# A one-core decoder layer: mixer C beside the stick-breaking passes, mixer A after them, and new tile pools

## Chip, core and metric

The kernel runs on one core of one Trainium2 chip. The metric is the device time of one execution in microseconds (us). Before the change it is 2517.34 us, the median of 3 runs (2516.91 to 2517.41).

## What is computed

One layer of a decoder over 2048 tokens of width 1024, in float32 throughout. Products that need full precision are made of high and low parts (three products with fp32r operands for one). The mixing half, cut to what matters here:

```python
h = _rmsnorm(x, norm_mix[l])
a_u, a_v, b_in, c_q, c_k, c_v, d_q, d_k, d_v = jnp.split(h @ w_in[l], splits, axis=-1)
y_a = _chunked_sgu(a_u, a_v, sgu_w[l], sgu_b[l])          # gelu, layer norm per head, 128x128 causal mix, gate
y_b = _multiscale_pool(b_in, pool_w[l], pool_scale[l])    # trailing means of 2, 4, 8, 16 tokens
y_c = _swa_sink_attention(c_q, c_k, c_v, swa_sinks[l], rel_bias)   # window of 128, softmax with a sink
y_d = _stick_breaking_attention(d_q, d_k, d_v)            # sigmoid(z) times a running product, causal, 4 heads
x = x + _rmsnorm(jnp.stack([y_a, y_b, y_c, y_d], 2), gain).reshape(B, S, D) @ w_out[l]
```

After it comes the feed-forward half: `x + (silu(h Wg) * (h Wu)) Wd` with its own normalisation, and a last normalisation.

## The kernel before

**Pieces.** The tokens stand in 4 chunks of 512 (c), 8 pieces of 256 (s) and 16 blocks of 128 (b). `stick(c, pair, q)` is one pass of the stick-breaking attention: the queries of one chunk and of one pair of heads (0 and 1, then 2 and 3) against all key chunks up to it. Its loop over head, key chunk and block makes a score tile z on PE (L302, L303), two sigmoids on ACT (L306, L309), on the diagonal two masks on POOL (L312), a running product pr by a scan on DVE (L315), the weights s (L320), their transposes tr on PE (L330), the high and low parts wt on ACT and DVE (L332, L333), and the products acc with the values (L341, L342). `finish` copies out a head's result (ysb, L353). There are eight passes, n = 0 to 7.

**What runs beside the passes.** `feed` is a generator that issues all other projections and mixers A, B and C; it yields after each step with a cost. `merge(main, fill, ratio)` takes one pass and, after each of its yields, as many steps of `feed` as `ratio` times the pass's cost. `upto(limit)` hands out steps up to a chunk mark. Marks 0 to 3 make keys, queries, values and mixer B for the first pair; from mark 4 on, `keys_queries` makes those of the second pair. Before the change `gate` places mixer A (`mixer_a`, `sgu`: a projection of 512 columns, `gelu`, a layer norm, four products m with the gate's weights, the store of u) beside passes 3 to 5; after mark 8 come mixer C's projections (st, stored in cd) and `attend(mixer_c())`, whose steps `swa(s)` load keys kr and queries qr, split them (ck on ACT and DVE, cq on POOL), make logits z into `block` (L447), take the maximum and the exponentials (L467), transpose them (trc), multiply with the values (o) and store. The few steps of it that fit run beside passes 6 and 7.

**After the passes.** `load_wo` loads the output weights by row group (oraw) and splits them into 16 tiles wo (L618 on ACT, L619 on DVE). `out_proj` goes over 16 blocks: `prepare` loads y (the four mixers' outputs) and xres, normalises y per mixer (squares L644, L648) and transposes it (`split_T`, L630, L632, L633); 48 products ops follow (L694 to L696), and the residual is added (L697); `finish` normalises the row for the feed-forward half, transposes it (L663) and stores it as hTd. From block 9 to 12 it also loads back and splits parts of hTd (b1, b2). Between its yields the main program takes steps of `attend`, at 0.60 of the cost, and as many as must be done before a block is prepared (`done`).

**Pools.** A tile pool hands out a number of buffers per tag (bufs); a tile waits for the one that had the buffer before it. `pp` and `fa` hold the tiles of `feed`, `ring` the 18 buffers of tag k4 that carry wo and later the whole feed-forward half, `p3` (ph3) the tiles of `out_proj`. In `fa` a large tile of tag wv is first the value weights, then six eighths of w_a, then mixer C's `block`, which is cut by hand into bias, two logit tiles, et and cv. y and b1 share a tag with 2 buffers, xres and b2 another with 2.

**Order of the instructions.** All this is the order of the program; a list scheduler then orders every engine's instructions by readiness as it estimates it, and each engine and the DMA queue (SP issues all loads and stores) run them in that order. Lines of the profile are those of the kernel before.

Of the kernel before, what the change touches and what calls it, by code (L numbers as in the profile page):

```python
# [15 lines left out]
P = 128  # L16
# [98 lines left out]
def _build(nc, tc, A, top):  # L115
# [42 lines left out]
    with ExitStack() as ph1:  # L158
# [59 lines left out]
        def split_w(src, name, tag="w", bufs=4, eng=G, k0=0, step=KT):  # L218

            _, kt, n = src.shape  # L220
            w = (fa if tag == "wv" else pp).tile([P, 2, kt, n], F32R, name=name, tag=tag, bufs=bufs)
# [174 lines left out]
        def mixer_c():  # L396
            sinks = fa.tile([P, 4], F32, name="sinks", bufs=1)
            load(sinks, A["swa_sinks"].broadcast_to([P, 4]))
            block = fa.tile([P, 24 * 256], F32, name="block", tag="wv", bufs=1)
            bias = block[:, 0:4 * 256].rearrange("p (h k) -> p h k", h=4)  # L400
            lgs = [block[:, (4 + 8 * i) * 256:(12 + 8 * i) * 256].rearrange("p (i h k) -> p i h k", i=2, h=4)
                   for i in range(2)]
            et = block[:, 20 * 256:22 * 256].rearrange("p (h k) -> p h k", h=2)
            cv = block[:, 22 * 256:22 * 256 + 3 * P].rearrange("p (b d) -> p b d", b=3)
            ck = fa.tile([P, 2, P + SUB], F32R, name="ck", tag="v", bufs=1)
# [5 lines left out]
            def bank(name):  # L411
                tag, n = {"z": (("mm", 2), ("z", 2)), "trc": (("ms", 1), ("ms", 1)),
                          "o": (("mm", 2), ("acc", 1))}[name][alone[0]]
                return psum.tile([P, CH], F32, name=name, tag=tag, bufs=n)
# [6 lines left out]
            def swa(s):  # L421
# [7 lines left out]
                lg = lgs[s % 2]  # L429
# [26 lines left out]
                nm = fa.tile([P, 2, 4], F32, name="nm", tag="nm")  # L456
# [3 lines left out]
                es = fa.tile([P, 2, 4], F32, name="es", tag="es")  # L460
# [3 lines left out]
                su = fa.tile([P, 2, 4], F32, name="su", tag="su")  # L464
# [6 lines left out]
                for i in range(2):  # L471
# [4 lines left out]
                    for g in range(2):  # L476
                        tr = bank("trc")
                        trv = tr.rearrange("p (h k) -> p h k", h=2)
                        for hd in range(2):
                            for u in blocks:  # L480
                                nc.tensor.transpose(trv[:, hd, u * P:(u + 1) * P],
                                                    lg[:, i, 2 * g + hd, u * P:(u + 1) * P], ident)
                        S.copy(et[:, :, r], trv[:, :, r])
# [125 lines left out]
        def load_wo():  # L609

            gout = ring.tile([P, KT], F32, name="gout", bufs=1)
# [23 lines left out]
        def out_proj(op, wo, put_h):  # L635
            def prepare(b):
                y = op.tile([P, D], F32, name="y", tag="y")
# [16 lines left out]
            def finish(b, y, xr):  # L654
# [25 lines left out]
            yield -NS  # L680
            ready = prepare(0)
            for b in range(NB):
                y, xr, yT = ready
                if b + 1 < NB:
                    if (b + 1) % 2 == 0:
                        yield (b + 1) // 2 - NS
                    ready = prepare(b + 1)
                    yield 0.9
# [32 lines left out]
        fas = ExitStack()  # L721
        fa = fas.enter_context(tc.tile_pool(name="feeda", bufs=2, side="right", reuse_waits="tile"))
        pp = fps.enter_context(tc.tile_pool(name="feed", bufs=2, side="right", reuse_waits="tile"))
        q, vts = {}, {}
        done, alone, projected = [0], [0], [0]

        def attend(swa):
            late = iter(())
            for s in range(NS):
                while projected[0] <= s:  # L730
                    yield 0.1
                now = swa(s)
                for cost in now:
                    yield cost
                    if cost == 0.0:
                        break
                yield from late
                done[0] = s
                late = now
            yield from late  # L740
            done[0] = NS
# [8 lines left out]
        def feed():  # L750
# [15 lines left out]
            for s in range(NS):  # L766
# [23 lines left out]
                if s == NS - 1:  # L790
                    w_a = [split_w(A["w_a"][:, 0:6], "w_a", "wv", 1)]
# [3 lines left out]
            w_a.append(split_w(A["w_a"][:, 6:8], "w_a", k0=6))  # L795
            w_c = [split_w(A["w_cm"][6], "w_c")]
            sgu = mixer_a()

            def wa(k, u):
                return w_a[k // 6][:, u, k % 6]  # L800
# [5 lines left out]
            late = [iter(())]  # L806

            def gate(s):
                now = sgu(s, hs[s], wa)
                for cost in now:  # L810
                    yield cost
                    if cost == 0.0:
                        break
                yield from late[0]
                late[0] = now

            yield ("chunk", NCH)
            q[NCH] = new_q()
            hs[1] = make_h(1)
            yield 0.5  # L820
            load_v(0)
            yield from keys_queries(NCH, 0, hs[0], stored_stats(0), w_k1, w_q1)
            yield from keys_queries(NCH, 1, hs[1], stored_stats(1), w_k1, w_q1)
            for s in range(2):
                yield from gate(s)
                hs.pop(s)
                hs[s + 2] = make_h(s + 2)
                yield 0.5
            for s in (2, 3):
                yield from gate(s)  # L830
            for c in range(1, NCH):
                yield ("chunk", NCH + c)
                q[NCH + c] = new_q()
                load_v(c)
                for s in (2 * c, 2 * c + 1):
# [254 lines left out]
```

## Time and profile before

| | |
|---|---|
| runs | 2516.91, 2517.34, 2517.41 us |
| the profiled execution | 2518.81 us |
| its span, first to last instruction | 2517.1 us |
| PE busy | 2286.6 us, 91% |
| DVE busy | 1623.0 us, 64% |
| ACT busy | 1048.7 us, 42% |
| POOL busy | 357.4 us, 14% |
| mean granted TensorE clock | 0.951 |

Busy times are averages over stages that differ, so the stages are read one by one: the windows view gives each engine's busy time in a stretch. A group's idle time tells how long its engine stood before it and who ended the wait. The chain of waits goes back from the last instruction, at each step to what released it. PE's times overlap each other, since products are pipelined; the granted clock says at which share of its full speed TensorE was allowed to run.

### The profile page before, as it was taken

The numbers are of one execution on the slowest core, as the hardware profiler recorded it, in microseconds if no ns is written. First come the engines' busy times: TensorE is split into PE (matmuls) and PEld (weight loads), VectorE is DVE, ScalarE is ACT, GpSimd is POOL, SyncE is SP. The second block draws the span as 40 slices with busy tenths as digits, with TensorE's granted clock in tenths as the row PEclk, the third lists the DMA queues.
The fourth block names the chain that finished last, engine by engine and source line by source line (L and its number), as shares of the span: only waits on it lengthen the run. The fifth ranks groups of instructions, "written<-read, shape, count | busy, mean of one in ns | idle before, by whom it ended". The sixth has DMA issues, their size and how long they took to land.

```text
span 2517.1 us, 30904 instructions
## 1 busy us (share of the span) xinstructions
PE 2286.6 (91%) x11308; PEld 1926.4 (77%) x11308; DVE 1623.0 (64%) x2634; ACT 1048.7 (42%) x2196; POOL 357.4 (14%) x372
## 2 busy tenths in 40 slices
PE   6989898897886888657999999999999999999998
PEld 6978776776875777545888888888888888888886
DVE  6688999898884543337666666655377666653443
ACT  5455566665654434234333333444233323332332
POOL 4232443454431210000000000000000000000000
PEclk9999999998996999878999999999999999999999
DMA  6232311222314333334222222556432222234553
GB/s 209 68 122 74 100 42 32 63 63 88 107 42 136 110 126 128 120 118 159 96 76 80 85 87 88 156 187 203 156 140 80 76 96 76 80 109 134 168 192 134
DMA packets 148808, 277.32 MB, mean 110 GB/s; under 512 B 12432, under 2 KB 84528, under 8 KB 148656
## 3 DMA queue, kind: packets, MB, share of 16 engines
q1 hardware_dynamic: 148656, 275.34, 32.9%
q8 instruction: 89, 1.46, 0.2%
q14 instruction: 63, 0.52, 0.1%
HBM read 211.60 MB, written 63.70 MB: 109 GB/s over the span
## 4 chain that ended last, share of the span: by engine, by line
PE 66%; DVE 15%; DMA 8%; issue 5%; ACT 3%; POOL 2%; SPq 0%; DVEq 0%; POOLq 0%; ACTq 0%
PE dn L1048 19%; PE gb L992 15%; PE gc L992 10%; PE ga L992 10%; DVE pr L315 4%; DVE s L320 3%; DMA qr<-cd 2%; DMA y<-yd 2%; DVE wt L333 1%; PE ops L694 1%; PE ops L695 1%; PE ps L242 1%; PE ps L243 1%; PE ops L696 1%; PE ps L244 1%
## 5 line engine op out<-in xcount | busy, mean ns | idle before, releaser
L1048 PE MATMUL dn<-wd,act 128*128 128x512 f32 x2112 | 479.5, 389 | 0.0
L1048 PEld LDWEIGHTS dn<-wd,act 128*128 128x128 f32 x2112 | 396.4, 188 | 82.5
L992 PE MATMUL gb<-T,fw 128*128 128x512 f32 x1584 | 387.9, 394 | 11.8 <-ACT fw L980 11.8
L992 PEld LDWEIGHTS gb<-T,fw 128*128 128x128 f32 x1584 | 298.8, 189 | 79.6 <-ACT fw L980 12.2
L992 PE MATMUL ga<-B,fw 128*128 128x512 f32 x1056 | 258.8, 393 | 0.0
L941 DVE TENSOR_TENSOR wd<-wr,wd 128x512 fp32r<-128x512 f32 x176 | 114.7, 689 | 215.4 <-ACT wd L1042 215.3
L992 PEld LDWEIGHTS ga<-B,fw 128*128 128x128 f32 x1056 | 198.6, 188 | 45.2
L145 POOL TENSOR_TENSOR fr<-rs_t,mhalf 128x1 f32<-128x1 f32 x32 | 20.3, 641 | 1449.4 <-DVE rs_t L144 1443.0
L1042 ACT CAST wd<-wr 128x512 fp32r<-128x512 f32 x176 | 101.4, 619 | 268.3 <-DMA wr<-in_w_down 242.2
L980 ACT CAST fw<-fsum 128x512 fp32r<-128x512 f32 x176 | 105.1, 620 | 200.4 <-PE gb L992 151.5
L315 DVE TENSOR_TENSOR_SCAN pr<-tfix,cr 128x513 f32<-128x513 f32 x96 | 134.3, 1406 | 11.1 <-ACT tfix L306 11.0
L213 POOL TENSOR_TENSOR h<-xr,h 128x1024 fp32r<-128x1024 f32 x47 | 122.1, 2607 | 112.1 <-ACT h L212 109.6
L992 PE MATMUL gc<-T,fw 128*128 128x512 f32 x528 | 134.1, 390 | 1.5 <-ACT fw L980 1.5
L992 PE MATMUL gc<-B,fw 128*128 128x512 f32 x528 | 130.3, 396 | 0.0
L941 DVE TENSOR_TENSOR fw<-fsum,fw 128x512 fp32r<-128x512 f32 x176 | 120.3, 687 | 11.6 <-ACT fw L980 10.0
L320 DVE TENSOR_TENSOR s<-s,pr 128x512 f32<-128x512 f32 (+3 forms) x152 | 122.8, 818 | 5.2 <-ACT s L309 1.2
L997 ACT COPY p<-gb 128x512 f32<-128x512 f32 x44 | 25.8, 585 | 227.1 <-PE gb L992 226.9
L992 PEld LDWEIGHTS gc<-B,fw 128*128 128x128 f32 x528 | 99.2, 188 | 24.0
L992 PEld LDWEIGHTS gc<-T,fw 128*128 128x128 f32 x528 | 99.2, 188 | 22.7 <-ACT fw L980 2.2
L330 PE MATMUL tr<-ident,s 128*128 128x128 f32 x544 | 97.2, 283 | 13.8 <-DVE s L320 7.7
L694 PE MATMUL ops<-wo,yT 128*128 128x512 f32 x256 | 106.8, 420 | 1.9 <-ACT yT L632 1.8
L941 DVE TENSOR_TENSOR fw<-fraw,fw 128x512 fp32r<-128x512 f32 x132 | 90.4, 687 | 26.1 <-ACT fw L980 26.1
(229 smaller groups left out, 4786.5 us busy)
## 6 DMA issues: line engine op xcount, KB each, us to landing
fraw<-in_w_gu SPq DMA_DIRECT2D x88, 512.0 KB
wr<-in_w_down SPq DMA_DIRECT2D x88, 512.0 KB
xr<-in_xT SPq DMA_DIRECT2D x48, 512.0 KB
actd<-up SPq DMA_DIRECT2D x88, 256.0 KB
ar<-actd SPq DMA_DIRECT2D x88, 256.0 KB
xt<-in_x SPq DMA_DIRECT2D x16, 512.0 KB
xres<-in_x SPq DMA_DIRECT2D x16, 512.0 KB
y<-yd SPq DMA_DIRECT2D x16, 512.0 KB
```

Of the source, the lines that this page charges most:

```text
L213: (V if q in on_v else G).tensor_tensor(h[:, :, 1], xr, h[:, :, 0].bitcast(F32), op=ALU.subtract)
L242: nc.tensor.matmul(o, w[:, 0, k], hk[:, 0], start=k == 0, stop=False)
L315: V.tensor_tensor_scan(pr[:, c0:][:, ::-1], t[:, c0:][:, ::-1], t[:, c0:][:, ::-1], carry[h][i], op0=ALU.mult, op1=ALU.bypass)
L320: (G if (4 * pair + c, i) in ON_G else V).tensor_tensor(w[:, c0:], w[:, c0:], pr[:, c0 + 1:], op=ALU.mult)
L330: nc.tensor.transpose(tr[:, i * P:(i + 1) * P], wq[i][:, col:col + P], ident)
L694: nc.tensor.matmul(ps, yk[:, 0, :], wo[k][half][:, 0], start=k == 0, stop=False)
L941: V.tensor_tensor(dst, src, hi.bitcast(F32), op=ALU.subtract)
L980: S.copy(w[:, 0], src)
L992: nc.tensor.matmul(bank, w[:, wi, sl], hc[n][:, k, hi], start=start and k + wi + hi == 0, stop=stop and k == 3 and wi == 1, skip_group_che ...
L997: S.copy(p6, bb)
L1042: S.copy(w[n][:, 0], wr[:, n])
L1048: nc.tensor.matmul(pss[2 * i + n], a[:, ai, t], w[n][:, wi], start=f + ai + wi == 0, stop=f == NF - 1 and ai == 1)
```

## The change

Mixer A leaves the passes: `gate` and its place in chunks 4 to 7 go, w_a is split into four tiles of tag w after mark 8, and A's eight pieces run after all of mixer C, four before mark 9 and four after it. Mixer C moves up: its three projections (`window`) follow the keys and queries of each chunk of the second pair, and steps of `attend` are taken three at a time after each of them (`beside`). `attend` no longer overlaps the end of one piece with the start of the next. `merge` gets other ratios and, for passes 6 and 7, ends at the next mark. After pass 7 the rest up to mark 9 is issued, `load_wo` takes one further step of `feed` per row group, and `out_proj` takes the steps that are left (A's last pieces) at 0.80 of its cost; `gated` says which pieces of A are done.

Pools: a pool `feedv` holds w_v alone and is closed after its last use; `feedw` takes its place with C's tiles, now separate, with one logit tile in place of two; w_c's third part gets its own buffer. et shares a buffer with mixer A's v, C's banks of PSUM change. `ring` has 16 buffers of k4 and 2 of a new tag raw, used by oraw, by b1 and b2 and later by ar. y has 3 buffers. `ph3` and the feed-forward pool change sides with `fh`, which is opened as soon as `feed` is used up.

The core of the diff:

```diff
 def mixer_c():
-            block = fa.tile([P, 24 * 256], F32, name="block", tag="wv", bufs=1)
-            lgs = [block[:, (4 + 8 * i) * 256:(12 + 8 * i) * 256].rearrange("p (i h k) -> p i h k", i=2, h=4)
-                   for i in range(2)]
+            bias = fw.tile([P, 4, 256], F32, name="bias")
...
-                lg = lgs[s % 2]
+                lg = fw.tile([P, 2, 4, 256], F32, name="lg", tag="lg")
+                cv = fw.tile([P, 3, P], F32, name="cv", tag="cv")
...
 def load_wo():
-                raw = ring.tile([P, 2, CH], F32, name="oraw", tag="k4")
+                raw = ring.tile([P, 2, CH], F32, name="oraw", tag="raw", bufs=2)
...
 def out_proj(op, wo, put_h):
-                y = op.tile([P, D], F32, name="y", tag="y")
+                y = op.tile([P, D], F32, name="y", tag="y", bufs=3)
...
-                    b1 = op.tile([P, 2, CH], F32, name="b1", tag="y")
+                    b1 = ring.tile([P, 2, CH], F32, name="b1", tag="raw", bufs=2)
-                    b2 = op.tile([P, 2, CH], F32, name="b2", tag="xres")
+                    b2 = ring.tile([P, 2, CH], F32, name="b2", tag="raw", bufs=2)
...
 def attend(swa):
-                now = swa(s)
-                for cost in now:
-                    yield cost
-                    if cost == 0.0:
-                        break
-                yield from late
+                yield from swa(s)
...
 def feed():
-            for s in range(2):
-                yield from gate(s)
...
+            sw = attend(mixer_c())
+
+            def beside(n):
+                for _ in range(n):
+                    cost = next(sw, None)
+                    if cost:
+                        yield cost
...
+            for c in range(NCH):
+                yield ("chunk", NCH + c)
+                q[NCH + c] = new_q()
...
+                for s in (2 * c, 2 * c + 1):
+                    yield from keys_queries(NCH + c, s, hs[s], rbcs[s % 2], w_k1, w_q1)
+                    yield from beside(3)
+                for s in (2 * c, 2 * c + 1):
+                    yield from window(s, hs.pop(s), rbcs[s % 2])
+                    n = (s + 2) % NS
+                    hs[n] = make_h(n)
+                    yield 0.5
+            yield ("chunk", 2 * NCH)
+            w_a = [split_w(A["w_a"][:, 2 * k:2 * k + 2], "w_a", k0=2 * k) for k in range(4)]
+            yield from sw
+            sgu = mixer_a()
...
+            for s in range(NS):
+                now = sgu(s, hs.pop(s), wa)
+                for cost in now:
+                    yield cost
+                    if cost == 0.0:
+                        break
+                yield from late
+                late = now
+                gated[0] = s
...
-        ratios = (38 / 10.8, 38 / 21.6, 38 / 32.4, 52 / 43.2, 4.00, 1.20, 1.00, 1.50)
+        ratios = (38 / 10.8, 38 / 21.6, 38 / 32.4, 38 / 43.2, 38 / 10.8, 38 / 21.6, 38 / 32.4, 52 / 43.2)
...
-            merge(stick(c, pair, q[n]), upto(n + 2 if n < 6 else 99), ratios[n])
+            merge(stick(c, pair, q[n]), upto(n + 2), ratios[n])
+        for _ in upto(2 * NCH + 1):
+            pass
+        fvs.close()
         ph1.close()
-        ring = top.enter_context(tc.tile_pool(name="ring", bufs=18, side="left", reuse_waits="tile"))
+        ring = top.enter_context(tc.tile_pool(name="ring", bufs=16, side="left", reuse_waits="tile"))
...
+        rest = upto(99)
+        for _ in load_wo():
+            next(rest, None)
...
-                    due = cost * 0.60
+                    due = cost * 0.80
...
-                    ar = pair("ar")
+                    ar = ring.tile([P, 2, CH], F32, name="ar", tag="raw", bufs=2)
```

How the order on the engines moves, at three places. The first is DVE in pass 3 (pr, s and wt are the pass). Before, mixer A stands among them (gq, mu, u, vs):

```order
L526 COPY u<-gq 128x256
L529 TENSOR_REDUCE mu<-gq 128x4
L320 TENSOR_TENSOR s<-s,pr 128x512
L530 TENSOR_SCALAR mu<-mu 128x4
L513 TENSOR_SCALAR gq<-gq 128x512
L532 TENSOR_TENSOR gq<-gq,mu 128x256
L514 TENSOR_TENSOR gq<-gq,xs 128x512
L333 TENSOR_TENSOR wt<-tr,wt 128x256
L333 TENSOR_TENSOR wt<-tr,wt 128x128
L315 SCALAR_TENSOR_TENSOR pr<-tfix_201,cr 128x513
L320 TENSOR_TENSOR s<-s,pr 128x512
L315 SCALAR_TENSOR_TENSOR pr<-tfix_200,cr 128x513
```

And after, in pass 4 with C's logits lg, the values put in place (vstack) and C's projections (st):

```order
L333 TENSOR_TENSOR wt<-tr,wt 128x512 x2
L443 SCALAR_TENSOR_TENSOR lg<-z,bias 128x512 x2
L286 SCALAR_TENSOR_TENSOR vstack<-vt,vstack 128x2x64
L333 TENSOR_TENSOR wt<-tr,wt 128x512
L315 SCALAR_TENSOR_TENSOR pr<-tfix_200 128x385
L286 SCALAR_TENSOR_TENSOR vstack<-vt,vstack 128x2x64
L315 SCALAR_TENSOR_TENSOR pr<-tfix_201 128x513
L320 TENSOR_TENSOR s<-s,pr 128x384
L333 TENSOR_TENSOR wt<-tr,wt 128x512
L320 TENSOR_TENSOR s<-s,pr 128x512
L803 TENSOR_TENSOR st<-ps,rbc 128x256
L315 SCALAR_TENSOR_TENSOR pr<-tfix_200 128x129
```

All of A's operations are gone from the passes; seven of C's eight pieces have all their logits lg placed before the last pr, where before the change it was two.

The second is DVE after the last pass. Before, the weights wo come among the pieces of C that are still to be done:

```order
L470 RECIPROCAL su<-su 128x8
L493 TENSOR_TENSOR block<-o,su 128x256
L619 SCALAR_TENSOR_TENSOR wo<-oraw,gout,wo 128x512 x4
L493 TENSOR_TENSOR block<-o,su 128x256
L619 SCALAR_TENSOR_TENSOR wo<-oraw,gout,wo 128x512 x2
L447 SCALAR_TENSOR_TENSOR block<-z,block 128x512 x2
L619 SCALAR_TENSOR_TENSOR wo<-oraw,gout,wo 128x512
L447 SCALAR_TENSOR_TENSOR block<-z,block 128x512
L423 CAST ck<-ck 128x2x128
L619 SCALAR_TENSOR_TENSOR wo<-oraw,gout,wo 128x512
L447 SCALAR_TENSOR_TENSOR block<-z,block 128x512
```

And after:

```order
L466 RECIPROCAL su<-su 128x8
L616 SCALAR_TENSOR_TENSOR wo<-oraw,gout,wo 128x512 x4
L490 TENSOR_TENSOR lg<-o,su 128x256
L616 SCALAR_TENSOR_TENSOR wo<-oraw,gout,wo 128x512 x9
L490 TENSOR_TENSOR lg<-o,su 128x256
L616 SCALAR_TENSOR_TENSOR wo<-oraw,gout,wo 128x512 x3
L510 TENSOR_SCALAR gq<-gq 128x512
L511 TENSOR_TENSOR gq<-gq,xs 128x512
L510 TENSOR_SCALAR gq<-gq 128x512
L511 TENSOR_TENSOR gq<-gq,xs 128x512
L523 COPY u<-gq 128x256
```

The wo conversions now all stand ahead of the first operation on gq, which is A's first piece; ACT's order is alike. On PE, 13 of A's 16 projections stand between here and the first product of the output projection.

The third is SP's queue in the output projection, from block 9 on. Before (b_10228 and b_10226 are b2 and b1 in the buffers of xres and y):

```order
L119 DMA y<-yd_65 128x1024
L119 DMA hTd_77<-hs 1024x1x128
L119 DMA x2d_74<-xres 128x1024
L119 DMA b_10228<-hTd_76 128x512
L119 DMA b_10226<-hTd_76 128x1024
L119 DMA hTd_77<-hs 1024x1x128
L119 DMA x2d_74<-xres 128x1024
L119 DMA y<-yd_65 128x1024
L119 DMA xres<-in_x 128x1024
L119 DMA b_10351<-hTd_76 128x512
L119 DMA b_10349<-hTd_76 128x1024
```

And after (b_10269 and b_10271 are b1 and b2 in the ring's own buffers):

```order
L119 DMA y<-yd_65 128x1024
L119 DMA hTd_76<-hs 1024x1x128
L119 DMA x2d_74<-xres 128x1024
L119 DMA b_10269<-hTd_76 128x1024
L119 DMA b_10271<-hTd_76 128x512
L119 DMA xres<-in_x 128x1024
L119 DMA y<-yd_65 128x1024
L119 DMA b_10392<-hTd_76 128x1024
L119 DMA hTd_77<-hs 1024x1x128
L119 DMA b_10394<-hTd_76 128x512
L119 DMA x2d_74<-xres 128x1024
```

The loads of b1 and b2 now stand ahead of the block's loads of xres and y and no longer take their buffers; the load of a second b1 comes already before the block's store of hTd.

## Rows read from the trace of the kernel before

**Rows 1.** windows view: window, PE, PEld, DVE, ACT, POOL, granted clock, DMA, GB/s

```profile
504.00:575.00 71.00, 60.65 (x359) 52.55 (x358) 67.03 (x111) 45.40 (x98) 40.23 (x35) 0.96 0.22 66
575.00:765.00 190.00, 159.29 (x1039) 141.93 (x1038) 157.72 (x203) 107.02 (x247) 67.81 (x67) 0.92 0.24 76
332.00:765.00 433.00, 370.52 (x2207) 319.25 (x2205) 382.06 (x590) 254.78 (x571) 185.57 (x179) 0.94 0.20 64
765.00:1173.00 408.00, 297.88 (x1481) 250.17 (x1482) 175.27 (x333) 157.20 (x412) 51.55 (x75) 0.83 0.41 135
1173.00:2517.00 1344.00, 1332.38 (x5808) 1091.71 (x5806) 797.92 (x1268) 456.34 (x839) 10.67 (x16) 1.00 0.35 118
```

**Rows 2.** tile view of ysb: its copies, ns min/median/max, first and last start

```profile
L353 ACT COPY ysb<-yp x16: 352/373/404, 119.5 to 765.5; 128x256 f32<-128x256 f32 x16
```

**Rows 3.** windows view of the tile gq alone: DVE, ACT, POOL

```profile
332.00:765.00 433.00, 50.24 (x94) 19.98 (x30) 35.38 (x32) 0.94 0.20 64
```

**Rows 4.** the same of the tile m: PE, PEld, DVE

```profile
332.00:765.00 433.00, 13.32 (x64) 10.76 (x64) 10.83 (x32) 0.94 0.20 64
```

**Rows 5.** the same of the tile vs: DVE

```profile
332.00:765.00 433.00, 10.97 (x32) 0.94 0.20 64
```

**Rows 6.** groups of DVE in 332:765: busy us, mean ns, idle before

```profile
L530 DVE TENSOR_SCALAR mu<-mu 128x4 f32<-128x4 f32 x16 | 8.0, 501 | 0.2
```

**Rows 7.** windows view of the tile block alone: PE, PEld, DVE, ACT

```profile
332.00:765.00 433.00, 0.95 (x4) 0.48 (x4) 9.97 (x12) 8.04 (x32) 0.94 0.20 64
765.00:1173.00 408.00, 58.27 (x368) 52.35 (x368) 35.90 (x46) 42.57 (x130) 0.83 0.41 135
```

**Rows 8.** the same of the tile ck

```profile
765.00:1173.00 408.00, 17.34 (x88) 15.11 (x88) 5.02 (x10) 3.08 (x5) 0.83 0.41 135
```

**Rows 9.** timeline of ACT after the last pass: start, us, what, idle before

```profile
779.64 1.33 ACT L618 ACTIVATE wo<-oraw,gout 128x512 fp32r<-128x512 f32 x2 [9.52 <-DMA oraw<-in_w_out]
...
782.23 1.34 ACT L618 ACTIVATE wo<-oraw,gout 128x512 fp32r<-128x512 f32 x2 [0.79 <-DMA oraw<-in_w_out]
...
815.56 1.32 ACT L618 ACTIVATE wo<-oraw,gout 128x512 fp32r<-128x512 f32 x2
```

**Rows 10.** groups of POOL in 332:765

```profile
L213 POOL TENSOR_TENSOR h<-xr,h 128x1024 fp32r<-128x1024 f32 x28 | 74.4, 2663 | 59.1 <-ACT h L212 58.9
...
L145 POOL TENSOR_TENSOR rv<-rs_t,mhalf 128x4 f32<-128x4 f32 x16 | 20.1, 1254 | 16.2 <-DVE rs_t L144 16.1
```

**Rows 11.** chain of waits in 750:800 and 1000:1080: start us, us, what

```profile
784.76 2.46 DMA yd<-block
...
1005.85 1.65 PE ytr L630 x8
...
1015.05 3.96 DMA y<-yd
...
1023.11 1.70 PE ytr L630 x8
...
1032.07 0.89 PE ytr L663 x8
...
1049.61 1.94 PE ytr L630 x8
...
1074.68 1.94 PE ytr L630 x8
```

**Rows 12.** tile view of v: ns min/median/max, first and last start

```profile
L540 DVE TENSOR_TENSOR v<-gq,rv x16: 406/420/2562, 350.2 to 563.6; 128x256 f32<-128x256 f32 x16
```

**Rows 13.** timeline of 1150:1176, the last addition and the first gate product

```profile
1154.54 0.69 DVE L697 TENSOR_TENSOR xres<-ops,xres 128x512 f32<-128x512 f32 x1 [1.93 <-PE ops L696]
...
1172.49 1.22 PE L992 MATMUL gb<-T,fw 128*128 128x512 f32 x2 [11.76 <-ACT fw L980]
```

**Rows 14.** waits in 575:765: total us, times, longest

```profile
POOL cq L437 <- DMA qr<-cd: 37.2, 8, 10.4
...
DVE pr L315 <- POOL tfix L312: 6.9, 3, 4.8
```

More of the change, by code (lines that the diff above doesn't have):

```diff
@@ L220, in split_w @@
             _, kt, n = src.shape
-            w = (fa if tag == "wv" else pp).tile([P, 2, kt, n], F32R, name=name, tag=tag, bufs=bufs)
+            w = (pp if tag == "w" else fv[0]).tile([P, 2, kt, n], F32R, name=name, tag=tag, bufs=bufs)
             per = min(kt, D // n, step)
@@ L463, in swa @@
                 S.activation(es, es, AF.Exp)
-                su = fa.tile([P, 2, 4], F32, name="su", tag="su")
+                su = fw.tile([P, 2, 4], F32, name="su", tag="su", bufs=2)
                 for i in range(2):
@@ L794, in feed @@
                     make_bias()
[L795 to L800, printed above, removed]
+            w_c = [split_w(A["w_cm"][6 + g], "w_c", ("w", "w", "wc")[g], (4, 4, 1)[g]) for g in range(3)]
             def load_v(c):
@@ L864, in feed @@
                     yield 0.5
-        sw = []
+                if s == 3:
+                    yield ("chunk", 2 * NCH + 1)
+            yield from late
+            gated[0] = NS
         source = feed()
@@ L893, in _build @@
         wo = []
-        rows = load_wo()
-        for _ in upto(99):
-            next(rows, None)
-            for _ in range(2):
-                next(sw[0])
-        for _ in rows:
-            pass
-        fps.close()
-        with tc.tile_pool(name="ph3", bufs=2, side="right", reuse_waits="tile") as p3:
-            fh = top.enter_context(tc.tile_pool(name="fh", bufs=1, side="left", reuse_waits="tile"))
-            hc = {n: fh.tile([P, 4, 2, CH], F32R, name=n) for n in ("T2", "B11", "T3", "T1")}
-            def put_h(n, k, src):
-                S.copy(hc[n][:, k, 0], src)
-                V.tensor_tensor(hc[n][:, k, 1], src, hc[n][:, k, 0].bitcast(F32), op=ALU.subtract)
-            gffn = fh.tile([P, D], F32, name="gffn", tag="g")
+        rest = upto(99)
@@ L915, in _build @@
                 if cost < 0.0:
-                    need = int(cost) + NS + 1
-                    while done[0] < need:
-                        next(sw[0], None)
+                    while gated[0] <= int(-cost - 1):
+                        if next(rest, None) is None:
+                            break
                 else:
-                    due = cost * 0.60
+                    due = cost * 0.80
                     while due > 0:
-                        due -= next(sw[0], 1e9)
-        fas.close()
+                        due -= next(rest, 1e9)
@@ L927, in _build @@
+                    if due < -1e8 and not hc:
+                        fps.close()
+                        fh = top.enter_context(tc.tile_pool(name="fh", bufs=1, side="right", reuse_waits="tile"))
+                        hc.update({n: fh.tile([P, 4, 2, CH], F32R, name=n) for n in ("T2", "B11", "T3", "T1")})
     with ExitStack() as ph4:
-        fp = ph4.enter_context(tc.tile_pool(name="fp", bufs=2, side="right", reuse_waits="tile"))
+        fp = ph4.enter_context(tc.tile_pool(name="fp", bufs=2, side="left", reuse_waits="tile"))
```

99 lines of the change are left out of this document (32 added, 67 removed).

## The prediction

> **What bounds the kernel now.** I read the windows view first, then DVE by group and by tile, then the chain of waits. [rows 1] splits the span where the stick-breaking passes end. The last pass ends at 765.5 us [rows 2]; the third of the eight ends near 332 us. In 332:765, five passes run beside mixer A and the projections of mixer C: DVE is busy 382.06 of 433 us, a share of 0.88. In 765:1173 come most of C and the output projection: PE is busy 298 of 408 us at a mean granted clock of 0.83, and no engine is full. From 1173 on the feed-forward part keeps PE busy 1332 of 1344 us. It is the same in both kernels except for two ring buffers that get a tag of their own; I take it as unchanged. So the change is worth what it does to two stages: the **pass stage** (433 us, bounded by DVE) and the **output stage** (408 us, bounded by waits).
>
> **The pass stage.** Of the two mixers, A leaves it and C comes in; the third pass and all before it keep their work, and I cost that at nothing. A's DVE work here: 50.24 us on the gelu tile [rows 3], 10.83 on the gate's products [rows 4], 10.97 on the variances [rows 5] and 8.0 for the means' scaling, L530 [rows 6], together 80 us. C's DVE work: 35.90 us on its block of logits now stands in the output stage beside 9.97 here [rows 7], and 5.02 us go to its keys there [rows 8], 50.9 us in all. The order puts seven of C's eight pieces ahead of the last scan: 7/8 x 50.9 less the 10 that were here already, so 34 us come in. Scaling A's weights also falls here now, 4 operations of about 1.2 us: 5 us. DVE has 382 - 80 + 34 + 5 = 341 us.
>
> How long that takes depends on how full DVE can be kept. The stretch 504:575 with A beside the pass has DVE busy 67.03 of 71 us, share 0.944; 575:765, with C's projections and the first quarter of its windows, 157.72 of 190, share 0.83 [rows 1]. After the change all the stretches look like the second, so I take 0.83: 341 / 0.83 = 411 us, **22 us saved**. The other end, 341 / 0.944 = 361 us, would save 72. The saving is smaller than 80 - 39 because C's chain is worse company than A's: its queries come by DMA, and POOL, which converts them, waits.
>
> **The output stage, step by step.** After the last pass four things come in a row.
>
> First the output weights. On ACT and on DVE the order places all sixteen conversions ahead of A's first operation, so A cannot start on its results before they are through. Before, the first conversion began 779.64 - 765.5 = 14 us after the pass, and the first rows followed each other by 2.6 us while nothing else held the loads [rows 2, 9]. There are two row buffers before and after. Eight rows: 14 + 7 x 2.6 = 33 us. The slow end is what the eight took before, beside C: the last began at 815.56, 51 us in all.
>
> Then A, alone. PE issues 13 of A's 16 projections before the first product of the output projection, and two fit into PSUM ahead of their evacuation, so 11 half steps, 5.5 of 8 steps, lie on the path. A step's engine time: PE 48 products of 1344 / 5808 = 0.231 us each [rows 1], 11.1 us; DVE 80 / 8 = 10 us; POOL 35.38 / 8 for the gelu product and square [rows 3], 20.1 / 8 for the power and 2 x 2.66 for h [rows 10], 12.3 us, the longest. The row buffer u is single, so a step also waits for the store of the one before: 2.46 us for a 256 KB store in its shortest row [rows 11]. 12.3 + 2.5 = 14.8 us a step, 81 us. The low end is POOL without gaps, 68 us.
>
> Here a rule bears on the price. DVE's v took 420 ns in the median and 2562 at most [rows 12], as if it had stood behind something. The Trainium skill, "SBUF — State Buffer", section "Who interferes with whom", says that a DVE instruction with two SBUF inputs and a GpSimd instruction that reads SBUF lock each other out for a whole instruction. By that rule POOL's and DVE's parts of a step would add up, as in the third rival below; the trace shows single cases, not how many of A's there would be.
>
> Then the output projection. Before, two things set its pace. y has two buffers, and a block's y can be loaded only when the block before last is through its transposes: the chain goes from the transposes over the load (3.96 us) to the next transposes, from 1005.85 to 1023.11, 17.3 us a block. And in four blocks b1 and b2 sit in the slots of y and xres, so that those blocks took 1074.68 - 1049.61 = 25.1 us [rows 11]. After, y has three buffers and b1 and b2 have two of the ring, so both waits go; what is late next is PE itself. A block is 48 products, 11.1 us; 16 transposes, 2 x 0.89 us [rows 11]; and about 1 us in which PE waits for ACT's copy of the transposed y, since they still stand directly ahead of the products: 13.9 us, 16 blocks 222 us. The rest of A among them adds 72 products, 17 us, and four blocks with b1 and b2 some 1.5 us each: 245 us.
>
> Last the way into the feed-forward part, 1154.54 to 1172.49, 18 us [rows 13]. The sixteen ring buffers are all weights now, so fewer of hb's loads can go ahead: 21 us.
>
> Sum: 33 + 81 + 245 + 21 = 380 us against 408, **28 us saved**. From both sides: 33 + 68 + (16 x 13 + 17) + 18 = 344 us at best, with 1 us less a block than above; at worst 51 us for the weights, 123 for A and 294 for the projection (both among the rivals) and 21, 489 us.
>
> **The sum.** 2517.1 - 22 - 28 = 2467 us of span. The profiled execution took 2518.81 us, 1.7 more than its span, and the median of the runs is 2517.34, 1.5 less than it; the two cancel, so 2467 us.
>
> **The rivals.**
>
> *C's loads hold the passes.* In 575:765 POOL waited 37.2 us for eight query loads, 4.65 us each, of which DVE was seen to wait 6.9 us behind POOL's masks [rows 14]. POOL works in order, and the masks of each pass's diagonal blocks stand behind the queries; so do PE's products for C, ahead of the passes' own. Now 28 such loads fall into the pass stage. If each reached DVE in full, the stage would be 341 + 28 x 4.65 = 471 us, 38 longer; with the 28 saved later 2517 + 38 - 28 = **2527 us, slower**. It decides from 4.5 us per load on (341 + 28 x 4.5 = 467, 34 longer). Against it: only 6.9 of 37.2 us came through before.
>
> *The output projection keeps its pace*, because the chain over ACT and POOL and not the y buffer sets it: 17.3 us a block, 16 x 17.3 + 17 = 294 us in place of 245, 2467 + 49 = **2516 us, no change**. For it: the rest of that chain goes over ACT, POOL, DVE and PE one after the other. Against: with three buffers it has two blocks' time.
>
> *POOL and DVE take turns in A*: 12.3 and 10 us add up to 22.3 us a step, 5.5 steps are 123 us in place of 81, 42 more, **2509 us**, little faster than before. For it: the long v. Against: the median of v is 420 ns, so at least half of the sixteen were not held.
>
> *Both stages fill*: DVE at 0.944 and the output stage at 344 us give 2517 - 72 - 64 = **2381 us**. For it: A's own stretch had that share. Against: it needs both.
>
> *Nothing moves as said*: the order excludes it, since A's products stand behind the passes.
>
> **Chances.** Forecast, with 2430 to 2500 us as its own range: 0.51. Both fill: 0.15. Turns: 0.10. Pace kept: 0.11. Loads hold: 0.09. The second and third together: 0.04. A measurement of this kernel can tell about 0.2%, 5 us. Turns lie below that line, so faster is 0.51 + 0.15 + 0.10 and 0.01 of pace kept, 0.77; same is the other 0.10 of it; slower 0.09 + 0.04, 0.13. The range leaves out the upper end of the best case and the worst pair: 2405 to 2526.
>
> **What would show it.** Right: between the third and the last pass about 411 us, DVE busy some 341 of them, and hardly an A product there; then about 33 us with PE mostly idle; A's steps 15 us apart; blocks of the output projection 14 us apart with a granted clock near 1. Wrong: PE or DVE waiting long for POOL's cq during the passes; blocks 17 us apart; y's load still on the chain; or a feed-forward part that is not 1344 us long.

## The result

The changed kernel takes 2561.8 us (median of 4 runs, 2558.2 to 2565.5), the kernel before 2517.4 us beside it (2516.9 to 2520.1): a ratio of 1.0174, 95% interval 1.0157 to 1.0192. It is slower, by 44 us; forecast were 2467 us, and the range ended at 2526. The profiled execution has a span of 2561.1 us, which the readings below use.

### The profile page after: what moved, and what is told of

It reads as the page before. It is cut to its first block, busy times and chain, and to the rows that moved or that the text cites. A ratio compares the mean times of both kernels' runs of the same rounds, so it can differ in the third digit from the quotient of the medians.

```text
span 2561.1 us, 31007 instructions
## 1 busy us (share of the span) xinstructions
PE 2326.6 (91%) x11308; PEld 1944.1 (76%) x11308; DVE 1623.3 (63%) x2634; ACT 1082.1 (42%) x2214; POOL 350.0 (14%) x372
## 4 chain that ended last, share of the span: by engine, by line
PE 66%; DVE 6%; DMA 5%; issue 3%; ACT 3%; POOL 1%; SPq 0%; DVEq 0%; POOLq 0%; ACTq 0%
PE dn L1031 19%; PE gb L975 14%; PE ga L975 10%; PE gc L975 9%; PE ops L691 2%; PE ops L692 2%; PE ops L693 2%; DVE pr L315 2%; PE ps L254 1%; PE ps L255 1%; PE ps L256 1%; DMA yd<-lg 1%; PE tr L330 1%; DMA cd<-st 1%; DVE s L320 1%
## 5 line engine op out<-in xcount | busy, mean ns | idle before, releaser
L320 DVE TENSOR_TENSOR s<-s,pr 128x512 f32<-128x512 f32 (+3 forms) x152 | 111.8, 746 | 11.0 <-ACT s L309 7.6
L330 PE MATMUL tr<-ident,s 128*128 128x128 f32 x544 | 110.7, 314 | 4.8 <-DVE s L320 4.2
L333 DVE TENSOR_TENSOR wt<-tr,wt 128x512 fp32r<-128x512 f32 (+3 forms) x160 | 94.3, 601 | 24.1 <-ACT wt L332 23.4
L332 ACT CAST wt<-tr 128x512 fp32r<-128x512 f32 (+3 forms) x160 | 81.9, 528 | 64.1 <-PE tr L330 60.5
L963 ACT CAST fw<-fraw 128x512 fp32r<-128x512 f32 x132 | 81.3, 619 | 61.0 <-DVE fw L924 32.4
```

The costliest lines, as they stand in the source:

```text
L320: (G if (4 * pair + c, i) in ON_G else V).tensor_tensor(w[:, c0:], w[:, c0:], pr[:, c0 + 1:], op=ALU.mult)
L330: nc.tensor.transpose(tr[:, i * P:(i + 1) * P], wq[i][:, col:col + P], ident)
L332: S.copy(wt[:, 0, r], tr[:, r])
L333: V.tensor_tensor(wt[:, 1, r], tr[:, r], wt[:, 0, r].bitcast(F32), op=ALU.subtract)
L963: S.copy(w[:, 0], src)
```

## The profile after

The windows view of the changed kernel, cut where the three stages end now: the third pass ends near 326 us, the last at 809.8, and the first feed-forward product starts at 1215. Columns: stretch, length, busy time of each engine with its instructions, granted clock, DMA share, GB/s.

```profile
326.00:810.00 484.00, 373.87 (x2166) 319.26 (x2164) 341.78 (x499) 279.01 (x650) 132.06 (x164) 0.81 0.18 55
810.00:1215.00 405.00, 338.35 (x1521) 272.39 (x1521) 212.69 (x430) 161.27 (x354) 102.53 (x92) 0.90 0.43 138
1215.00:2561.00 1346.00, 1335.82 (x5808) 1092.90 (x5808) 805.55 (x1265) 464.68 (x839) 12.36 (x16) 1.00 0.36 118
```

Against [rows 1]: the pass stage went from 433 to 484 us, with less DVE work (341.78 us in place of 382.06). DVE's share fell from 0.88 to 0.71 and no engine is full. PE's busy time there has not fallen (373.87 us after 370.52), while its granted clock went from 0.94 to 0.81; with a share of 0.77 PE is now the busiest engine of the stage. The output stage has hardly moved, 408 to 405 us, and the feed-forward part, 1344 to 1346, not at all. The last two passes carry the loss: before, they took 190 us together (575:765 in [rows 1]); now they take 127 and 126 us.

```profile
557.00:684.00 127.00, 98.33 (x606) 85.90 (x604) 83.88 (x126) 69.30 (x164) 27.09 (x42) 0.84 0.17 52
684.00:810.00 126.00, 96.18 (x472) 76.37 (x472) 99.74 (x123) 76.28 (x170) 50.05 (x42) 0.74 0.19 59
```

The waits of DVE in the pass stage of the changed kernel (who waited for whom: total us, times, longest) begin with one that DVE did not have in this stage before: the logits of mixer C wait for the store of an earlier window, since its result is written into the logits tile lg, and lg is now single.

```profile
DVE lg L443 <- DMA yd<-lg: 26.7, 4, 11.3
DVE su L465 <- ACT lg L463: 18.5, 7, 3.9
DVE pr L315 <- POOL tfix L312: 16.9, 6, 6.1
...
DVE wraw L227 <- DMA wraw<-in_w_a: 10.4, 3, 6.8
```

The kernel before writes C's result into its logits tile too. It has two of them, and most of its windows run after the passes; there, in 765:1173, DVE waited for the same kind of store:

```profile
DVE block L447 <- DMA yd<-block: 24.8, 5, 7.9
```

So the change brought this wait into the passes, where it stands ahead of their own work; it did not create it.

In the output stage ACT's conversions of the weights end at 837.6 us, 28 us after the last pass; A then runs alone until the first product of the output projection at 940.6, 103 us; the last addition ends at 1193.3, and 22 us later the feed-forward part starts. The chain of waits shows a step of A (start, us, what; lines in between left out):

```profile
867.02 1.21 DVE v L537
868.52 4.27 DMA yd<-u
872.89 0.51 DVE u L523 x2
873.49 0.36 DVE u L544
873.89 0.80 PE m L543 x2
874.69 0.43 PE ps L254
...
889.51 2.56 DMA yd<-u
...
909.84 2.72 DMA yd<-u
...
929.77 2.12 DMA yd<-u
```

The stores of the rows u start 20 to 21 us apart: that is A's step, which the prediction had at 14.8 us.

## Experiments

Each ratio stands against the kernel before, run beside it. "Pass stage" is the time from 326 us (332 in the kernels made from the one before) to the end of the last pass. The third pass itself ends between 321 and 330 us in the kernels made from the changed one, and at 340 us in no_a, so stages that differ by some 5 us are not told apart.

### The two halves of the exchange apart

**c_after** writes all of mixer C behind the last pass:

```
 def beside(n):
-    for _ in range(n):
-        cost = next(sw, None)
-        if cost: yield cost
+    yield from ()
...
+yield ("chunk", 2 * NCH + 1)
 yield from sw
```

> The changed kernel with all eight windows of mixer C run after the last pass instead of beside the passes; its three projections and A's weights stay where the change put them. Theory 1 (C's chain of small steps holds the passes: it sits in the in-order queues of PE, DVE, ACT and SP ahead of the passes' own work): the pass stage, 484 us with C, falls by far more than C's 34 us of DVE work, to 400 us or less, and C alone afterwards takes 8 x 12 to 8 x 20 = 100 to 160 us. Theory 2 (C is innocent; without A's work DVE is no longer what bounds the passes, and the projections on PE at a lowered clock do): the pass stage stays at 450 us or above and the total grows by about C's time alone, to 2640 us or more.

2567.3 us, ratio 1.0208 (1.0193 to 1.0223).

```profile
326.00:694.00 368.00, 306.18 (x1886) 263.40 (x1884) 306.86 (x438) 242.28 (x551) 116.63 (x133) 0.86 0.19 58
694.00:810.00 116.00, 60.20 (x253) 51.51 (x254) 38.52 (x68) 38.98 (x104) 17.76 (x31) 0.50 0.25 77
```

The stage falls by 116 us, to 368, with DVE at 0.83, the very share of the prediction. But it isn't free of C: the maxima (nm) of four of the eight windows lie ahead of the last pass's end all the same, since the scheduler pulled ready work forward. The rest then costs 116 us alone with PE at half clock, about what the passes had gained. Theory 1 holds for the stage; the total hardly cares where C stands (1.0208 after 1.0174).

**no_a** takes mixer A out of the kernel before:

```
-now = sgu(s, hs[s], wa)
...
+G.memset(u, 1.0)
+store_y(s, 0, 256, u)
```

> The kernel before without mixer A: its eight windows are left out and a constant is stored for its quarter of y; the weights of A are still split. Its 80 us of DVE work leave the pass stage (433 us) and nothing comes in. Theory 1 (DVE bounds the passes, as the prediction had it): the stage falls to (382 - 80) / 0.83 = 364 us, at most 380. Theory 2 (with A gone the passes run into another bound, their own chain and the projections on PE): the stage falls by less than 30 us, to 403 us or more, and DVE's share there falls to 0.75 or less.

2453.7 us in one run, 60 less than before; the pass stage is 367 us (358 from the end of its own third pass), close to theory 1's 364. A's leaving was worth what the prediction said. That DVE alone bounded the passes isn't shown by it: A leaves every engine, and PE's busy time in the stage fell from 370.52 to 294 us as well. C then brought in 117 us (484 - 367), of which the forecast had 44 (411 - 367).

### What C costs beside the passes

**own_row** gives C's result a tile of its own:

```
+yo = pp.tile([P, 2, 256], F32, name="yo", tag="cw", bufs=1)
-V.tensor_tensor(lg[:, i, 0]..., ob, sb_, op=ALU.mult)
+V.tensor_tensor(yo[:, i]..., ob, sb_, op=ALU.mult)
-store_y(s, 512, 768, lg[:, :, 0])
+store_y(s, 512, 768, yo)
```

> The changed kernel with mixer C's result written into a row tile of its own instead of into its logits, so that the next window's logits need not wait for the store. Theory (the single logits tile costs the passes what DVE waited for that store, 15.4 us in the sixth pass alone): those waits go and the total falls by 8 to 15 us, to about 2550 us. Rival (DVE waits there for work that is late anyhow): the total stays within 5 us of 2562.

2528.8 us, ratio 1.0056 (1.0038 to 1.0074): 33 us less by the medians, 30 by the ratios, more than the wait itself. DVE's wait for the store has left its list, whose first lines are now:

```profile
DVE wt L333 <- ACT wt L332: 20.2, 22, 2.1
DVE su L465 <- ACT lg L463: 18.5, 5, 5.0
```

The stage is 450 us. That it gains more than 26.7 us fits engines that work in order: on PE, C's products z and the projections (ps) behind them waited 13.8 and 10.7 us for DVE's lg in the changed kernel; in own_row the first wait is gone and the second is 5.8 us. The edit shows that C's result in the logits tile was the trouble; whether a second logits tile would have done as well wasn't tried.

**spread** divides the softmax step (after es, and after each four exponentials, a `yield 0.45`), on top of own_row:

> own_row with mixer C's step of a maximum and eight exponentials divided into four steps, so that the passes' work can be placed between. Theory (that lump, 8 x 0.7 us on ACT with table loads, holds DVE's sum and ACT's own work for the passes; DVE waited 18.5 us for it): the total falls by 8 to 15 us from 2528.8. Rival (lumps are broken up by the scheduler as it is): within 5 us.

2518.2 us, ratio 0.9987 (0.9978 to 0.9997); 17 us less by the ratios; the stage falls to 431 us. The lump was in the way.

**no_loads** and **rest** leave out the loads of C's keys and queries, from own_row and from spread:

```
-load(kr[:, g], both_halves(cd[s][0, g * HD:(g + 1) * HD, :]))
+V.memset(kr, 0.01)
...
-load(qr[:, hd], both_halves(cd[s][1 + g, hd * HD:(hd + 1) * HD, :]))
+V.memset(qr, 0.01)
```

> own_row with the loads of mixer C's keys and queries left out: their tiles are set to a constant on DVE instead (48 loads go, 24 short DVE operations come in). Theory (C's chain holds the passes by its loads, which come 7 to 9 us after they are issued and which POOL, and PE behind it, wait for): the pass stage falls from own_row's 450 us to 420 or less, total 2499 or less. Rival (the loads are hidden; the chain of C's arithmetic, ACT's exponentials above all, sits in the queues): the stage stays at 440 or above, total 2519 or above.

2515.6 us in one run, stage 434 us: 16 us for the loads, between the two theories.

> spread with the loads of mixer C's keys and queries left out as in no_loads (constants in their place). Pass stages so far: 484 us in the changed kernel, 450 with the row tile of its own (own_row), 431 with the divided exponentials too (spread), 434 in no_loads, 368 without C (c_after). If the store, the exponentials and the loads are three prices that add up, the stage falls to 450 - 19 - 16 = 415 us, and what is left over 368 is C's own DVE work at the old share, 36 / 0.83 = 43 us. If exponentials and loads are one and the same wait, it stays at 428 to 434 us, and 60 us of C's price are still without a name.

2522.1 us in one run, 1.003 of the one run of the kernel before beside it, stage 438 us. The prices don't add up: without the loads the division of the exponentials gains nothing (434 us in no_loads). That both mend the same idle time fits this, but one run each doesn't show it.

**no_c**, **half1** and **half2** leave out the whole of C's chain, its second half, and its first, from own_row.

> own_row without mixer C's attention: a constant is stored for its quarter of y; C's three projections stay. It gives the pass stage without any of C's chain. If C's price in own_row (450 us) is no more than its DVE work of 66 us at full occupation, the stage is 384 us or more; if C costs more than its work (in-order queues, waits), 365 us or less.

> own_row with the first half of mixer C alone (keys, queries, logits); softmax, transposes and values are left out and a constant is stored. Theory 1 (the first half, with its loads by DRAM and POOL's conversions, carries the price): the stage is within 20 us of own_row's 450 us. Theory 2 (the second half carries it: exponentials, transposes and values on ACT and PE, one after the other): within 20 us of no_c.

> own_row with the second half of mixer C alone: the logits are a copy of the bias (four DVE copies a window, no keys, no queries, no products z, no loads of C but its values). Theory 2 (see half1): the stage is within 20 us of own_row's 450 us; theory 1: within 20 us of no_c. If both halves lie in the middle, each carries its own work and neither is the cause alone.

In one run each: 2366.4, 2454.0 and 2433.8 us. Their pass stages (396, 480 and 461 us) can't be compared, and so don't decide between the theories: with less of C ahead of it, A was pulled into the passes (its first operations at 556, 678 and 678 us in place of 804). The totals can: all of C costs 162 us, taking out the second half gives back 75, the first 95, together 170. Neither half is the cause alone. C's 162 us stand against 58 us of DVE's busy time and 112 us of PE's (the pages' totals of own_row less those of no_c): its chain is dearer than its work on any one engine. Which queue charges how much of it stays open beyond the store. C's PSUM banks, which the change also moved, and the end of one window, which no longer overlaps the start of the next, weren't tried apart.

**mix** puts C behind the passes, two windows after each of A's first four (with own_row's, spread's and gate3's edits; C's et and A's m take other buffers):

> The repairs (own row tile, divided exponentials, one bank for m, single u) with mixer C written behind the passes: two of its windows after each of A's first four, so that the scheduler may pull C ahead of them only where its inputs are ready. Theory (C costs the passes by standing ahead of their work in the order; behind it, it fills gaps, and A and C fill each other's): pass stage 370 to 400 us, C and A together 150 to 170 us, total 2440 to 2475 us. Rival (C behind the passes is C alone, as in c_after, whose windows then took 25 us each): total 2510 or above.

2654.7 us, ratio 1.0556 (1.0538 to 1.0573), a clear miss. The stage came to 382 us, as the theory had it; but 301 us lie between the last pass and the first product of the output projection.

```profile
700.00:850.00 150.00, 60.97 (x255) 49.33 (x253) 56.54 (x102) 44.81 (x98) 35.38 (x40) 0.58 0.23 71
```
```profile
POOL cq L433 <- DMA qr<-cd: 55.1, 8, 39.2
```

C's and A's windows, taken in turn and whole, don't cover each other: in 150 us PE is busy 61, and POOL waits for C's query loads.

### A alone

**gate2** adds a second u to own_row:

```
-u = pp.tile([P, 2, 256], F32, name="u", tag="u", bufs=1)
+u = (fa if s % 2 else pp).tile([P, 2, 256], F32, name="u", tag=("u", "vt")[s % 2], bufs=1)
```

> own_row with a second row buffer u for mixer A (its windows take turns between two tiles). In the changed kernel A's steps came 20.4 us apart after the passes, where the prediction had 14.8: DVE waited for the store of u, ACT behind it kept the PSUM banks, PE stood still for some 7 us a step, and its next products were granted 1.2 GHz. Theory (the single u and the clock that falls in its wait cost 5 us and more a step): the steps shrink to 14 to 16 us and the total falls by 20 to 30 us from own_row's 2528.8, to about 2503. Rival (the chain over POOL, or the single v, sets the step in any case): at most 8 us are gained.

2525.6 us, ratio 1.0019 (1.0009 to 1.0029), 9 us less by the ratios. A alone (from ACT's last conversion of the weights to the first product of the output projection) takes 97.8 us, after 103.3 in own_row: nearly the rival.

**gate3** puts the four products m into one bank:

```
+m = psum.tile([P, CH], F32, name="m", tag="ms", bufs=1)
+ms = [m[:, hd * P:(hd + 1) * P]... for hd in range(4)]
+for hd in range(4):
+    nc.tensor.matmul(ms[hd], sgw[:, hd, :], v[:, :, hd * HD:(hd + 1) * HD], start=True, stop=True)
 for hd in range(4):
     r = slice(hd * HD, (hd + 1) * HD)
-    m = psum.tile([P, CH], F32, name="m", tag="ms", bufs=1)
```

> gate2 with the four heads' products m of a window of mixer A in four quarters of one PSUM bank, issued one behind the other, in place of four passages through one bank in which each waits for DVE's addition of the head before. In gate2 the steps still come 17 to 20 us apart; PE waits 10.9 us for DVE's u in 100 us, its clock then stands at 1.2 GHz for the next products. Theory (this to-and-fro between PE and DVE sets the step, with the clock that falls in it): steps of 14 to 15 us, 15 to 20 us less in all than gate2 (ratio to before 0.994 to 0.996). Rival (DVE's work in order, the power on POOL and v behind it, sets the step): at most 5 us less.

2515.5 us, ratio 0.9982 (0.9972 to 0.9992), again 9 us, between the two expectations; A alone takes 86.6 us. PE's waits in that phase, first of the changed kernel (838 to 940 us), then of gate3 (807 to 893):

```profile
PE m L543 <- DVE u L544: 12.2, 8, 3.3
PE ps L254 <- ACT gq L509: 5.3, 3, 3.3
PE m L543 <- DVE v L537: 4.8, 1, 4.8
```
```profile
PE ps L254 <- ACT gq L510: 6.9, 3, 3.9
PE m L543 <- DVE v L538: 6.2, 2, 5.4
```

The to-and-fro over one bank is gone; what is left waits for ACT's gq and for v. **repairs** joins it with spread:

> gate3 with the divided softmax step of spread: the changed kernel with all repairs found so far (own row tile for C's result, divided exponentials, two u, one bank for m). If the repairs add up: own_row 1.0056, less 0.007 for the exponentials, 0.004 for u and 0.004 to 0.007 for the bank: 0.988 to 0.991, some 2492 us. If they repair the same waits: 0.995 or above.

2495.9 us, ratio 0.9908 (0.9893 to 0.9922): these add up. So mended, the change is faster than the kernel before. But by3b below, which has the output projection's buffers and leaves A and C where they were, stands at 0.9779: the exchange itself still costs some 32 us.

### The output projection's part alone

**by3** is the kernel before with a third buffer for y (b1 shares it), and a ring of 17.

> The kernel before with one edit of the change alone: y gets a third buffer in the output projection (one ring buffer less for it). Theory (the load of y set the pace of 17.3 us a block): blocks come 14 to 15 us apart, 12 to 16 of them, so the total falls by 30 to 45 us, to 2472 to 2487. Rival (C's steps between the blocks set the pace; the 14.2 us of the changed kernel come from C being gone): blocks stay at 17 us and the total within 8 us of 2517.

2470.9 us, ratio 0.9824 (0.9809 to 0.9838). **by3b** moves b1 and b2 into C's block tile:

```
-b1 = op.tile([P, 2, CH], F32, name="b1", tag="y", bufs=3)
+if k == 0:
+    bb.append(fa.tile([P, 2, 2, 2, CH], F32, name="bb", tag="wv", bufs=1))
+b1, b2 = bb[0][:, k % 2, 0], bb[0][:, k % 2, 1]
```

> by3 (the kernel before with a third buffer for y) with b1 and b2 of the output projection in the tile that mixer C has left by then, instead of in slots of y and xres. Theory (in those four blocks the load of y still waits for b1's slot, and the block takes 18 to 20 us instead of 14): 4 x 4 to 4 x 6 us are gained, total 2447 to 2455. Rival (the loads of b1 and b2 behind the store of hTd set these blocks): at most 5 us.

2463.8 us, ratio 0.9779 (0.9762 to 0.9795), the fastest of all: 11 us less by the ratios, where 16 to 24 were expected. The residual's additions (tile xres on DVE: count; ns min/median/max; first and last start) give the pace, for the kernel before, by3, by3b and the changed one:

```profile
L697 DVE TENSOR_TENSOR xres<-ops,xres x16: 680/688/693, 999.8 to 1154.5; 128x512 f32<-128x512 f32 x16
```
```profile
L697 DVE TENSOR_TENSOR xres<-ops,xres x18: 684/692/692, 967.2 to 1103.3; 128x512 f32<-128x512 f32 x18
```
```profile
L701 DVE TENSOR_TENSOR xres<-ops,xres x18: 680/691/693, 966.2 to 1094.5; 128x512 f32<-128x512 f32 x18
```
```profile
L694 DVE TENSOR_TENSOR xres<-ops,xres x18: 683/692/692, 978.5 to 1098.1; 128x512 f32<-128x512 f32 x18
```

There are two additions a block. The first one of the last block starts at 1150.7, 1098.0, 1090.5 and 1094.5 us, 7 blocks behind the first start in the kernel before and 8 in the others: 21.6 us a block before, 16.4 in by3, 15.5 in by3b, 14.5 after. In by3's chain the load of y still stands behind that of b in three of these blocks, two of which are shown; in by3b's chain it doesn't stand any more.

```profile
1006.51 2.52 DMA b<-hTd
...
1011.15 3.41 DMA y<-yd
...
1024.68 2.73 DMA b<-hTd
...
1029.54 3.40 DMA y<-yd
```

**by3c** adds the edits of spread and gate3 to by3b:

> by3b (the kernel before with the output projection's buffers) with the divided exponentials and the single bank for m as well. There A runs beside the passes and C's softmax mostly beside the output projection. If the two edits help in that order too: 5 to 15 us less than by3b (ratio 0.972 to 0.976). If both only mend what the change had brought (A alone on PE, C beside the scans): within 5 us of by3b's 0.978.

2483.5 us, ratio 0.9857 (0.9842 to 0.9873): 20 us slower than by3b, outside both expectations. The passes end 13 us later and the output stage is 8 us longer. Which of the two edits does it wasn't tried.

## Why the prediction was wrong

- **The pass stage: the step that failed.** A's price was right (no_a). DVE's sum was right too (341 us forecast, 341.78 measured), in part by luck: by DVE's groups in the stage, C's operations add up to 65.7 us after 17.0, so that 49 us came in and not 34, while the passes' own operations took less, s above all (the kernel before, then the changed one: busy us, mean ns, idle before):

```profile
L320 DVE TENSOR_TENSOR s<-s,pr 128x512 f32<-128x512 f32 (+2 forms) x98 | 81.1, 841 | 3.7 <-ACT s L309 1.2 <-POOL s L312 1.0
```
```profile
L320 DVE TENSOR_TENSOR s<-s,pr 128x512 f32<-128x512 f32 (+2 forms) x98 | 70.7, 736 | 9.3 <-ACT s L309 7.6
```

  "After the change all the stretches look like the second, so I take 0.83" was not right: the share came out as 0.71, 484 us for 411. The 0.83 came from a stretch with two of C's windows and two logits tiles; the change brought all eight, ahead of the passes' own work, on one logits tile. The diff showed that tile and I costed the wait for the store from it at nothing. This wait alone was 34 us of the 73 (own_row), and the undivided softmax, which the kernel before had as well, 16 to 19 more (spread). The rest, some 20 us, stays open. PE stood in no term of the sum: it is busy 348 us of spread's 431, a share of 0.81, against 0.77 for DVE, and whether it holds the passes there wasn't tried.
- **A alone.** 81 us forecast, 103 measured. The term that failed is the step of 14.8 us, taken as the longest engine's sum plus a store. The four products m through one bank, each after DVE's work on the head before, and the store of u came in a row with the projections: 20.4 us, some five steps of it in the 103. With both mended (gate3) A alone took 86.6.
- **The weights.** 33 us forecast, 28 measured; the term was a little too large.
- **The output projection.** 245 us forecast, 252.7 measured; a block 13.9, measured 14.5 at a granted clock of 0.97 (941 to 1193 us). Right. The rival "keeps its pace" fell: y is off the chain. by3 shows that the third buffer works without the rest of the change, and was worth 43 us there.
- **The way into the feed-forward part**, 21 us, measured 22; the part itself unchanged. Right.
- **The sum**: 73 + 22 - 5 + 8 + 1 = 99 us too little in the terms; the stage begins 6 us earlier than before and the feed-forward part is 1.5 longer, which leaves the miss of 94 us.
- **The rival "C's loads hold the passes"** had the right side, and its 471 us were near the 484, by luck: they are DVE's bare 341 us and the loads, with no other wait. Its mechanism was the smaller part: taking the loads out gives 16 us (no_loads), the logits tile's store gave 34, and PE waited for POOL's cq 7.8 us in the whole stage of the changed kernel. I gave it 0.09, and the range ended 1 us below its 2527.
- **"POOL and DVE take turns in A"** had 22.3 us a step, near the measured 20.4, but gate3 shows that most of the excess wasn't that: there four of the ten v's of this phase were held, some 9 us in all, where the rival had 42.

The exchange as a whole: A cost the kernel before 60 us beside the passes (no_a) and costs 103 alone. C, of which six windows of eight ran after the passes before, costs 162 us in its new place (own_row against no_c); what it cost in the old one wasn't tried. The output projection's gain, 43 us by itself (by3), went into that.

## What to carry to other kernels

A chain of small dependent steps can cost more than its busy time on any one engine (here 162 us, for 112 on PE and 58 on DVE): price it by an experiment of leaving it out, or by the share of a stretch that already holds all of it, and add up every engine's work, not only that of the one that is fullest now. When a result is written into a tile that the next step needs again, list who waits for its last reader, a store above all, and what stands behind that wait on its engine. When an edit has separable parts, run the cheap part alone: here one buffer for y gave nearly what the whole rebuilding was forecast to give (43 us of 50).

## What the runs showed of the hardware

DVE's v takes 0.42 us in some windows and some 2.6 us in others. The timeline of the changed kernel shows why: a long v starts just behind POOL's h and ends just behind it.

```profile
869.07 2.33 POOL L213 TENSOR_TENSOR h<-xr,h 128x1024 fp32r<-128x1024 f32 x1
869.13 2.56 DVE L537 TENSOR_TENSOR v<-gq,rv 128x256 f32<-128x256 f32 x1 [0.64 <-POOL rv L145]
871.74 0.58 PE L543 MATMUL m<-v,sgw 128*128 128x128 f32 x1 [4.83 <-DVE v L537]
```

v ends at 871.69, h at 871.40. The Trainium skill, "SBUF — State Buffer", section "Who interferes with whom", has a DVE instruction with two SBUF inputs and a GpSimd (POOL) instruction that reads SBUF contend for a shared port pair, which one of them holds for the whole instruction. For h the rows agree. For POOL's rv, which reads SBUF too, they don't: in gate3 a v began within the second of two rv, 1.0 us each, and took 0.42 us (POOL's row, then DVE's):

```profile
851.16 1.98 POOL L145 TENSOR_TENSOR rv<-rs_t,mhalf 128x4 f32<-128x4 f32 x2 [0.17 <-DVE rs_t L144]
852.20 0.42 DVE L538 TENSOR_TENSOR v<-gq,rv 128x256 f32<-128x256 f32 x1 [0.55 <-POOL rv L145]
```

A v of 2.56 in place of 0.42 us, at the end of a wait of PE's of 4.83 us, is the part of the rival "take turns" that is real.

PE then pays again: behind that wait its next products are granted the lower level, 1.2 GHz. The windows view of the changed kernel in tens of microseconds (clock in the third column from the right) shows it in two steps of A in a row:

```profile
870.00:880.00 10.00, 6.90 (x20) 5.45 (x21) 6.80 (x13) 2.98 (x6) 4.79 (x4) 0.58 0.66 218
880.00:890.00 10.00, 9.26 (x47) 7.51 (x45) 5.74 (x15) 5.32 (x12) 6.25 (x6) 1.00 0.00 1
890.00:900.00 10.00, 6.73 (x19) 5.36 (x19) 6.71 (x13) 4.84 (x14) 5.60 (x4) 0.66 0.61 185
900.00:910.00 10.00, 8.82 (x47) 7.33 (x46) 5.51 (x18) 3.85 (x5) 6.21 (x6) 1.00 0.06 14
```

In the step at 874.69 ten products follow each other by 0.43 us, at a granted clock of 0.51 in 874.70:878.50, before the rest come every 0.23: 2 us a step on top of the wait.
